# Output projection and the values of two attention branches with 512 moving columns, summed over two halves of the rows

## The chip, the cores and the metric

The kernel runs on one core of a Trainium2 chip. The metric is the device time of one execution in microseconds (us), as the median of several runs; the profile is that of one execution.

## What is computed

One layer of a decoder trunk over 2048 tokens of width 1024, in float32. Cut to what matters here:

```
h    = rmsnorm(x, norm_attn)
proj = h @ w_in                       # 2048x1024 @ 1024x2700, columns split into q, k, v of four branches
o_A  = stick_breaking(qa, ka, va)     # 4 heads of 64: va is 256 columns wide, from column 512
o_B  = native_sparse_attention(...)   # compressed, selected and window parts, gates
o_C  = differential_attention(qc, kc, vc)   # 4 heads, vc is 256 columns wide, from column 1932
o_D  = sliding_window(qd, kd, vd)
mix  = concat(rmsnorm(o_A), rmsnorm(o_B), rmsnorm_per_head(o_C), rmsnorm(o_D))    # 2048x1024
x    = x + (mix * g_mix) @ w_out      # the output projection, 1024x1024
x    = x + relu(rmsnorm(x, norm_mlp) @ w_up)**2 @ w_down
out  = rmsnorm(x, norm_final)
```

## The kernel before

Every float32 product is made of three fp32r products: each operand is split into a high and a low part, and hi\*hi, lo\*hi and hi\*lo are summed in PSUM. So a product over 1024 rows is 8 row blocks of 128 times 3 = 24 matmuls into one PSUM tile.

The tokens go in four chunks c of 512, each of four blocks i of 128. There are two kinds of dense phase. P (`proj`, line 559) projects a chunk with `w_in`; M (`mlp`, line 608) does a chunk's output projection and MLP. The dense stream (`dense`, line 711) runs P0 to P3 and then M0 to M3. The chunk's input, transposed and split, lies in the two tiles `T_hi` and `T_lo`, which `put_T` (line 535) fills block by block.

In P the list `ORDER` (line 62) says which columns follow which. The q and k columns (`MT`) have the weights stationary and `T` moving with 512 columns; the v columns (`NG`) have a block of `T` stationary and the weights moving: 256 columns for `vA` and for `vC`, 268 for `vBD`. Of a v group, ScalarE (`evac`) copies each of the four blocks from PSUM into a tile of the ring `u_lo` (3 buffers), and SP issues the store to `nat_vA`, `nat_vC` or `nat_vBD` in DRAM. `vA` comes first, `vC` tenth in chunk 0 and last in the others, `vBD` last in chunk 0 and before `qD0` in the others.

In M the output projection (lines 620 to 634) takes four passes d of 256 columns. A pass needs two weight tiles of 128x1024, and for each block i it issues 24 matmuls with 256 moving columns; VectorE adds the PSUM tile to `acc`, which holds x (lines 631 and 632). After the last pass a block is normed (`sources`, `norm`), scaled, transposed and put into `T`, and the MLP follows.

Weights come through two `raw` buffers; ScalarE copies the tile to `w_hi`, GpSimd or VectorE subtracts into `w_lo` (`split_weights`, line 411); there are 3 pairs of these (`WB`), held from the first use to the last one of a group. M0 stores the split tiles to DRAM, and M1 to M3 load them from there, without a split, into the three pairs and the two `raw` buffers.

Beside the dense stream runs the attention: scores (PSUM tiles `z`), transposes (`t`), value products (`o`), chunk by chunk in the order A, C, D, B. A planner (`Plan`, `run`) interleaves the streams: it keeps its own estimate of when each operand is ready and issues an attention instruction on TensorE when it is due, and a dense one otherwise. Its price for a matmul is the moving columns divided by 2400 us (line 294): 0.107 us for 256, 0.213 us for 512. M0 begins once all branches of chunk 0 are stored; M3 needs the attention to be over. Dense PSUM tiles (`pd`) have 3 buffers, whatever part of the 512 columns is used.

Of the kernel before, what the change touches and what calls it, by code (L numbers as in the profile page):

```python
# [9 lines left out]
F32 = mybir.dt.float32  # L10
F32R = mybir.dt.float32r
U32 = mybir.dt.uint32
AF = mybir.ActivationFunctionType
OP = mybir.AluOpType
# [5 lines left out]
D = 1024  # L20
# [34 lines left out]
}  # L55

NG = {
    "vA": [(512, 256)],
    "vC": [(1932, 256)],
    "vBD": [(1216, 64), (1344, 76), (2572, 128)],  # L60
}
ORDER = (["vA", "qA0", "qA1", "kA0", "kA1", "qC0", "qC1", "kC0", "kC1", "vC",
# [3 lines left out]


def dap(t, off, dims):
    return bass.AP(tensor=t.tensor, offset=t.offset + off, ap=dims)
# [128 lines left out]
class Trunk:  # L198
# [135 lines left out]
    def weight_specs(self):  # L334
        def w_in(cols, k0, kn):
            wd = sum(w for _, w in cols)
            parts, o = [], 0
            for c0, w in cols:
                def place(t, o=o, w=w):
                    return t[:, :kn * wd].rearrange("p (k w) -> p k w", k=kn)[:, :, o:o + w]  # L340

                parts.append((place, dap(self.w_in, k0 * 128 * IN_COLS + c0,
                                         [[IN_COLS, 128], [128 * IN_COLS, kn], [1, w]])))
                o += w
            return parts

        def up(ft):
            return [(lambda t: t.rearrange("p (k w) -> p k w", k=KD),
                     dap(self.w_up, ft * 128, [[FF, 128], [128 * FF, KD], [1, 128]]))]

        for kind, c in self.phases:
            if kind == "P":
                for m in ORDER[c > 0]:
                    if m in MT:
                        yield kind, c, w_in(MT[m], 0, KD)
                    else:
                        kn = WMAX // sum(w for _, w in NG[m])
                        for k0 in range(0, KD, kn):
                            yield kind, c, w_in(NG[m], k0, min(kn, KD - k0))
            elif c:  # L360
                for j in range(8 + 2 * FF // 128):
                    yield "S", c, j
            else:
                for d in range(4):
                    for kk in range(2):
                        yield kind, c, [(lambda t: t.rearrange("p (k w) -> p k w", k=4),
                                         dap(self.w_out, kk * 512 * D + d * 256, [[D, 128], [128 * D, 4], [1, 256]]))]
                yield kind, c, up(0)
                yield kind, c, up(1)
                for fc in range(FF // 128 // FC):  # L370
                    if FC * fc + 2 < FF // 128:
                        yield kind, c, up(FC * fc + 2)
                    for f in range(FC):
                        yield kind, c, [(lambda t: t, dap(self.w_down, (fc * FC + f) * 128 * D, [[D, 128], [1, D]]))]
                    if FC * fc + 3 < FF // 128:
                        yield kind, c, up(FC * fc + 3)
# [182 lines left out]
    def proj(self, c):  # L559
# [4 lines left out]
        for m in order:  # L564
# [23 lines left out]
            else:  # L588
                wd = sum(w for _, w in NG[m])
                kn = WMAX // wd  # L590
                ws = yield from self.weights(-(-KD // kn))
                ws = [[t.rearrange("p (k w) -> p k w", w=wd) for t in w] for w in ws]
                for i in range(4):
# [11 lines left out]
            self.stored[m] = c  # L605
        self.fill += 1

    def mlp(self, c):

        dn = self.dn  # L610
# [6 lines left out]
            self.ld(a, dap(self.x, (c * 512 + i * 128) * D, [[D, 128], [1, D]]))  # L617
            acc.append(a)
        hh, hl = self.T
        for d in range(4):  # L620
            ws = yield from self.weights(2)
            for i in range(4):
                ts = slice(i * 128, i * 128 + 128)
                ops = []
                for k in range(KD):
                    wh, wl = [w[:, 256 * (k % 4):256 * (k % 4) + 256] for w in ws[k // 4]]
                    ops += [(a[:, k, ts], b) for a, b in ((hh, wh), (hl, wh), (hh, wl))]
                ps = yield from self.group(lambda p: p[:, :256], ops, (i, i + 1), used=d == 3)
                if i == 3:
                    self.res["w"].give(2)  # L630
                a = acc[i][:, d * 256:d * 256 + 256]
                V.tensor_tensor(a, a, ps[:, :256], OP.add)
                if d == 3:
                    self.added[c] = acc[:i + 1]
        self.fill += 1
        us = {}
# [238 lines left out]
    def loads_A(self, c, i, w0):  # L875
        for pr in range(2):
# [2 lines left out]
                yield from self.load_k(("kA", c, pr, j), f"kA{pr}", j, 0, c + 1)  # L879
            yield from self.load_q(("qA", c, pr, 1), f"qA{pr}", i + 2)  # L880
            for j in range(2):
                yield from self.load_v(("vA", c, pr, j), "vA", 128 * pr + 64 * j, 0, c + 1)

    def loads_B(self, c, i, w0):
        for pr in range(2):
# [8 lines left out]
    def loads_C(self, c, i, w0):  # L894
        for h in range(4):
# [2 lines left out]
            for mp in range(2):  # L898
                yield from self.load_k32(("kC", c, h, mp), f"kC{pr}", 2 * j + mp, c + 1)
            yield from self.load_q32(("qC", c, h, 1), f"qC{pr}", 2 * j, i + 2)  # L900
            yield from self.load_v(("vC", c, h), "vC", 64 * h, 0, c + 1)

    def loads_D(self, c, i, w0):
        for pr in range(2):
# [117 lines left out]
    def scores(self):  # L1022
        while self.filled[3] == 0:
            yield None
        self.attention_constants()
        yield from self.await_stored("vA", 0)
        for c in range(NC):
            for g in GROUPS:
                if g == "D":
# [653 lines left out]
```

## Time and profile before

| | us |
|---|---|
| median of 3 runs | 3088.4 (3086.42 to 3092.4) |
| the profiled execution | 3088.61 |
| its span, first instruction to last | 3086.8 |
| TensorE busy | 2995.2 (97%), 18951 matmuls |
| VectorE busy | 1860.2 (60%) |
| ScalarE busy | 1565.2 (51%) |
| mean granted clock | 0.993 of full speed |

A row's busy time of TensorE counts a matmul from its start to its modelled end, about 0.16 to 0.17 us after the next one could start; what a matmul takes of the engine is therefore read from the distance between two starts. "Idle before" is the idle time of the engine just before the instructions of a row, with what ended it.

### The profile page before, as it was taken

The numbers are of one execution on the slowest core, as the hardware profiler recorded it, in microseconds if no ns is written. First come the engines' busy times: TensorE is split into PE (matmuls) and PEld (weight loads), VectorE is DVE, ScalarE is ACT, GpSimd is POOL, SyncE is SP. The second block draws the span as 40 slices with busy tenths as digits, with TensorE's granted clock in tenths as the row PEclk, the third lists the DMA queues.
The fourth block names the chain that finished last, engine by engine and source line by source line (L and its number), as shares of the span: only waits on it lengthen the run. The fifth ranks groups of instructions, "written<-read, shape, count | busy, mean of one in ns | idle before, by whom it ended". The sixth has DMA issues, their size and how long they took to land.

```text
span 3086.8 us, 50946 instructions
## 1 busy us (share of the span) xinstructions
PE 2995.2 (97%) x18951; PEld 2513.8 (81%) x18951; DVE 1860.2 (60%) x4193; ACT 1565.2 (51%) x3195; POOL 449.7 (15%) x397
## 2 busy tenths in 40 slices
PE   8999999999999999999999999999999999999998
PEld 7788887788887777879888777879888888888887
DVE  4665658666656888787554778677654444432323
ACT  4654667554555776655544677545544443221111
POOL 2142323222222222221000000011000000110000
PEclk9999999999999999999999999999999999999999
DMA  7668555669556657877334545565553433645554
GB/s 205 197 202 219 169 165 146 180 185 260 176 195 211 200 183 237 269 243 227 111 139 139 167 148 159 173 198 160 190 158 131 149 123 123 247 163 206 186 204 157
DMA packets 396600, 563.01 MB, mean 182 GB/s; under 512 B 123712, under 2 KB 283584, under 8 KB 394688
## 3 DMA queue, kind: packets, MB, share of 16 engines
q1 hardware_dynamic: 396352, 559.75, 57.0%
q8 instruction: 150, 2.46, 0.3%
q14 instruction: 98, 0.80, 0.1%
HBM read 430.57 MB, written 129.07 MB: 181 GB/s over the span
## 4 chain that ended last, share of the span: by engine, by line
PE 73%; DVE 11%; ACT 7%; DMA 5%; issue 3%; POOL 1%; SPq 1%; DVEq 0%; POOLq 0%; ACTq 0%
PE pdM L296 42%; PE pdP L296 11%; DVE row L117 7%; ACT row L117 4%; PE zB L296 4%; PE tB L300 4%; PE oB L296 4%; PE oC L296 2%; PE tC L300 2%; PE zC L296 2%; DVE acc L117 1%; DMA raw<-in_w_in_dram 1%; DMA out_dram<-acc 1%; PE zD L296 1%; DMA acc<-in_x_dram 1%
## 5 line engine op out<-in xcount | busy, mean ns | idle before, releaser
L117 DVE TENSOR_TENSOR acc<-acc,pdM 128x512 f32<-128x512 f32 (+1 forms) x576 | 372.4, 654 | 229.8 <-PE pdM L296 200.8
L296 PE MATMUL pdM<-T_hi,w_hi 128*128 128x512 f32 (+1 forms) x1040 | 402.2, 387 | 0.7 <-DVE acc L117 0.7
L296 PE MATMUL pdM<-T_lo,w_hi 128*128 128x512 f32 (+1 forms) x1040 | 400.9, 386 | 0.0
L296 PE MATMUL pdM<-T_hi,w_lo 128*128 128x512 f32 (+1 forms) x1040 | 400.5, 385 | 0.0
L117 POOL TENSOR_TENSOR w_lo<-raw,w_hi 128x1024 fp32r<-128x1024 f32 (+2 forms) x92 | 227.7, 2478 | 441.7 <-ACT w_hi L117 375.8
L117 ACT ACTIVATE row<-row 128x1024 f32<-128x1024 f32 (+7 forms) x290 | 229.9, 805 | 108.9 <-DVE row L117 103.5
L296 PE MATMUL pdM<-raw,u_hi 128*128 128x512 f32 x720 | 281.4, 392 | 0.1
L296 PE MATMUL pdM<-w_hi,u_hi 128*128 128x512 f32 x664 | 268.8, 408 | 10.8 <-DVE acc L117 8.1
L296 PE MATMUL pdM<-w_hi,u_lo 128*128 128x512 f32 x664 | 263.8, 397 | 0.0
L296 PE MATMUL pdM<-w_lo,u_hi 128*128 128x512 f32 x664 | 263.3, 397 | 0.2 <-POOL w_lo L117 0.2
L117 ACT ACTIVATE r<-pdM 128x512 f32<-128x512 f32 x128 | 75.9, 593 | 353.3 <-PE pdM L296 351.7
L117 DVE TENSOR_TENSOR u_lo<-r,u_hi 128x512 fp32r<-128x512 f32 x128 | 93.0, 726 | 266.4 <-ACT u_hi L117 266.4
L117 ACT ACTIVATE PT<-tB 128x512 f32<-128x512 f32 (+1 forms) x244 | 130.2, 556 | 192.6 <-PE tB L300 190.9
L296 PEld LDWEIGHTS pdM<-T_hi,w_lo 128*128 128x128 f32 x1040 | 195.9, 188 | 36.7 <-issue 0.2
L296 PEld LDWEIGHTS pdM<-T_hi,w_hi 128*128 128x128 f32 x1040 | 196.0, 188 | 36.6 <-DVE acc L117 0.9
L117 ACT ACTIVATE row<-row,c_mn 128x1024 f32<-128x1024 f32 (+4 forms) x192 | 171.5, 895 | 106.0 <-DVE c_mn L117 104.7
L296 PEld LDWEIGHTS pdM<-T_lo,w_hi 128*128 128x128 f32 x1040 | 196.0, 188 | 35.7 <-issue 0.2
L117 ACT ACTIVATE w_hi<-raw 128x1024 fp32r<-128x1024 f32 (+2 forms) x160 | 164.6, 1036 | 116.9 <-DMA raw<-in_w_in_dram 47.5
L296 PE MATMUL pdP<-T_lo,w_hi 128*128 128x512 f32 x480 | 190.1, 396 | 0.0
L296 PE MATMUL pdP<-T_hi,w_hi 128*128 128x512 f32 x480 | 190.0, 396 | 0.0
L296 PE MATMUL pdP<-T_hi,w_lo 128*128 128x512 f32 x480 | 189.6, 395 | 0.0
L117 ACT ACTIVATE row<-row,b_mw 128x640 f32<-128x640 f32 (+7 forms) x160 | 134.6, 842 | 100.9 <-DVE b_mw L117 97.0
(224 smaller groups left out, 6948.7 us busy)
## 6 DMA issues: line engine op xcount, KB each, us to landing
w_hi<-w SPq DMA_DIRECT2D x162, 512.0 KB, 3.5
w_lo<-w SPq DMA_DIRECT2D x162, 512.0 KB, 4.4
raw<-w SPq DMA_DIRECT2D x108, 512.0 KB, 6.2
raw<-in_w_in_dram SPq DMA_DIRECT2D x72, 512.0 KB, 4.8
w<-w_hi SPq DMA_DIRECT2D x72, 512.0 KB, 3.0
w<-w_lo SPq DMA_DIRECT2D x72, 512.0 KB, 3.8
acc<-in_x_dram SPq DMA_DIRECT2D x32, 512.0 KB, 4.3
raw<-in_w_up_dram SPq DMA_DIRECT2D x32, 512.0 KB, 6.0
```

The costliest lines, as they stand in the source:

```text
L117: return f(*a, **k)
L296: self.nc.tensor.matmul(out, a, b, start=start, stop=stop, **k)
L300: self.nc.tensor.transpose(out, a, self.ident[:a.shape[0], :a.shape[0]])
```

## The change

`vA` and `vC` become one group `vAC` of 512 columns, first in both orders; in the chunks after the first, `vBD` moves to the end. A weight tile of `vAC` holds 2 row blocks of 512 columns (two DMAs of 256 KB) instead of 4 of 256, so the group needs four tiles. It is done in two halves `kh` of the 1024 rows: in the first half each block's 12 matmuls of 512 columns are copied by ScalarE into one of four tiles, two of `u_hi` and two of `u_lo`; in the second half VectorE adds the PSUM tile to that tile, and then it is stored, 512 columns wide.

The output projection takes two passes d of 512 columns, each in two halves of the rows. For each block a half is 12 matmuls of 512 columns instead of 24 of 256, and VectorE adds 512 columns to `acc` each time. The count of passes (4), of weight tiles (8), of PSUM groups (16) and of adds (16) per chunk stays.

```
 NG = {
-    "vA": [(512, 256)],
-    "vC": [(1932, 256)],
+    "vAC": [(512, 256), (1932, 256)],
     "vBD": [(1216, 64), (1344, 76), (2572, 128)],
 }
-ORDER = (["vA", "qA0", "qA1", "kA0", "kA1", "qC0", "qC1", "kC0", "kC1", "vC",
+ORDER = (["vAC", "qA0", "qA1", "kA0", "kA1", "qC0", "qC1", "kC0", "kC1",
           "qB0", "qB1", "kvcmp", "kB", "qD0", "qD1", "kD", "vBD"],
-         ["vA", "kvcmp", "qA0", "qA1", "kA0", "kA1", "qC0", "qC1", "kC0", "kC1",
-          "qB0", "qB1", "kB", "vBD", "qD0", "qD1", "kD", "vC"])
+         ["vAC", "kvcmp", "qA0", "qA1", "kA0", "kA1", "qC0", "qC1", "kC0", "kC1",
+          "qB0", "qB1", "kB", "qD0", "qD1", "kD", "vBD"])
...
-                for d in range(4):
-                    for kk in range(2):
-                        yield kind, c, [(lambda t: t.rearrange("p (k w) -> p k w", k=4),
-                                         dap(self.w_out, kk * 512 * D + d * 256, [[D, 128], [128 * D, 4], [1, 256]]))]
+                for d in range(2):
+                    for kk in range(4):
+                        yield kind, c, [(lambda t: t.rearrange("p (k w) -> p k w", k=2),
+                                         dap(self.w_out, kk * 256 * D + d * 512, [[D, 128], [128 * D, 2], [1, 512]]))]
...
+                if m == "vAC":
+                    yield from self.proj_halves(c, m)
+                    continue
...
+    def proj_halves(self, c, m):
+
+        hh, hl = self.T
+        out = []
+        for kh in range(2):
+            ws = yield from self.weights(2)
+            ws = [[t.rearrange("p (k w) -> p k w", k=2) for t in w] for w in ws]
+            for i in range(4):
+                ts = slice(i * 128, i * 128 + 128)
+                ops = []
+                for k in range(4):
+                    wh, wl = [w[:, k % 2, :] for w in ws[k // 2]]
+                    ops += [(a[:, 4 * kh + k, ts], b) for a, b in ((hh, wh), (hl, wh), (hh, wl))]
+                ps = yield from self.group(lambda p: p, ops, (i, i + 1))
+                if kh == 0:
+                    out.append(self.tile(self.dn, [128, 512], F32R, ("u_hi", "u_lo")[i % 2], 3).bitcast(F32))
+                    self.evac(out[i], ps)
+                else:
+                    self.V.tensor_tensor(out[i], out[i], ps, OP.add)
+                    self.st(self.v_d[m][c * 512 + i * 128:c * 512 + i * 128 + 128, :], out[i])
+            self.res["w"].give(2)
+        self.stored[m] = c
...
-        for d in range(4):
+
+        for d, kh in ((d, kh) for d in range(2) for kh in range(2)):
             ws = yield from self.weights(2)
+            end = d + kh == 2
             for i in range(4):
                 ts = slice(i * 128, i * 128 + 128)
                 ops = []
-                for k in range(KD):
-                    wh, wl = [w[:, 256 * (k % 4):256 * (k % 4) + 256] for w in ws[k // 4]]
-                    ops += [(a[:, k, ts], b) for a, b in ((hh, wh), (hl, wh), (hh, wl))]
-                ps = yield from self.group(lambda p: p[:, :256], ops, (i, i + 1), used=d == 3)
+                for k in range(4):
+                    wh, wl = [w[:, 512 * (k % 2):512 * (k % 2) + 512] for w in ws[k // 2]]
+                    ops += [(a[:, 4 * kh + k, ts], b) for a, b in ((hh, wh), (hl, wh), (hh, wl))]
+                ps = yield from self.group(lambda p: p, ops, (i, i + 1), used=end)
                 if i == 3:
                     self.res["w"].give(2)
-                a = acc[i][:, d * 256:d * 256 + 256]
-                V.tensor_tensor(a, a, ps[:, :256], OP.add)
-                if d == 3:
+                a = acc[i][:, d * 512:d * 512 + 512]
+                V.tensor_tensor(a, a, ps, OP.add)
+                if end:
                     self.added[c] = acc[:i + 1]
```

The rest of the diff renames `vA` and `vC` to `vAC` where the attention loads its values; they are read from one DRAM tensor of 512 columns instead of two of 256.

## Rows read from the trace of the kernel before

**Rows 1.** Page, part 1: busy us (share of the span), instructions of an engine.

```profile
PE 2995.2 (97%) x18951; PEld 2513.8 (81%) x18951; DVE 1860.2 (60%) x4193; ACT 1565.2 (51%) x3195; POOL 449.7 (15%) x397
```

**Rows 2.** Page, part 4: the chain that ended last, shares by engine and line.

```profile
PE 73%; DVE 11%; ACT 7%; DMA 5%; issue 3%; POOL 1%; SPq 1%; DVEq 0%; POOLq 0%; ACTq 0%
```

**Rows 3.** TensorE groups by shape: count, busy us, mean ns, idle before and its releasers.

```profile
L296 PE MATMUL pdM<-w_hi,T_hi 128*128 128x256 f32 x416 | 120.0, 289 | 3.8 <-DVE acc L117 3.7
...
L296 PE MATMUL pdP<-w_hi,T_hi 128*128 128x256 f32 x256 | 76.3, 299 | 6.6 <-DVE acc L117 3.6 <-ACT T_hi L117 2.4 <-DVE u_lo L117 0.6
...
L296 PE MATMUL pdM<-raw,T_hi 128*128 128x256 f32 x192 | 40.3, 285 | 0.6 <-DVE nx L117 0.6
...
L296 PE MATMUL pdM<-raw,T_lo 128*128 128x256 f32 x96 | 27.2, 284 | 0.0
```

**Rows 4.** TensorE timeline, output projection of M3: start us, us, instruction.

```profile
2675.02 0.28 PE L296 MATMUL pdM<-w_hi,T_lo 128*128 128x256 f32 x1
...
2684.02 0.28 PE L296 MATMUL pdM<-w_hi,T_lo 128*128 128x256 f32 x1
```

**Rows 5.** TensorE timeline, q and k columns of P0.

```profile
31.80 0.39 PE L296 MATMUL pdP<-T_hi,w_lo 128*128 128x512 f32 x1
...
53.35 0.39 PE L296 MATMUL pdP<-T_lo,w_hi 128*128 128x512 f32 x1
```

**Rows 6.** Stretches: length, busy us (instructions) of PE, PEld, DVE, ACT, POOL; clock, DMA share, GB/s.

```profile
2676.00:2711.00 35.00, 35.00 (x294) 35.00 (x293) 7.80 (x18) 0.73 (x2) 0.55 (x1) 1.00 0.79 295
2760.00:3040.00 280.00, 280.00 (x1237) 232.03 (x1236) 87.21 (x130) 48.42 (x78) 0.00 (x0) 1.00 0.53 192
0.00:700.00 700.00, 670.20 (x4313) 566.31 (x4314) 443.78 (x1056) 414.12 (x909) 198.26 (x186) 1.00 0.66 186
700.00:2618.00 1918.00, 1873.02 (x12410) 1564.69 (x12409) 1251.23 (x2865) 1060.57 (x2126) 232.81 (x190) 0.99 0.55 179
...
708.00:808.00 100.00, 90.99 (x762) 86.06 (x762) 62.42 (x180) 48.62 (x117) 30.16 (x24) 0.95 0.85 260
```

**Rows 7.** VectorE groups by shape.

```profile
L117 DVE TENSOR_TENSOR acc<-acc,pdM 128x512 f32<-128x512 f32 x512 | 346.0, 684 | 174.5 <-PE pdM L296 172.7
...
L117 DVE TENSOR_TENSOR acc<-acc,pdM 128x256 f32<-128x256 f32 x64 | 26.5, 417 | 55.4 <-PE pdM L296 28.2 <-DMA acc<-in_x_dram 23.6 <-PE pdM L300 3.0
```

**Rows 8.** ScalarE groups by shape.

```profile
L117 ACT ACTIVATE w_hi<-raw 128x1024 fp32r<-128x1024 f32 x148 | 155.0, 1055 | 105.5 <-DMA raw<-in_w_in_dram 44.0 <-PE pdP L296 16.7 <-PE pdM L296 15.9
...
L117 ACT ACTIVATE r<-pdM 128x512 f32<-128x512 f32 x128 | 75.9, 593 | 353.3 <-PE pdM L296 351.7 <-DVE u_lo L117 1.5
...
L117 ACT ACTIVATE u_lo<-pdP 128x256 f32<-128x256 f32 x32 | 11.9, 373 | 0.4 <-PE pdP L296 0.4
```

**Rows 9.** Page, part 5: the split on GpSimd.

```profile
L117 POOL TENSOR_TENSOR w_lo<-raw,w_hi 128x1024 fp32r<-128x1024 f32 (+2 forms) x92 | 227.7, 2478 | 441.7 <-ACT w_hi L117 375.8
```

**Rows 10.** The chain in order of time, 2610 to 2740 us: start us, us, what.

```profile
2624.80 29.96 PE pdM L296 x132
...
2669.49 47.34 PE pdM L296 x378
...
2716.86 0.42 DVE acc L117
```

**Rows 11.** Instructions on the tensor nat_vC: duration ns min/median/max, first and last start us.

```profile
L252 SPq DMA_DIRECT2D nat_vC<-u_lo x16: 319/350/1428, 93.5 to 711.5; - x16
L252 SPq DMA_DIRECT2D v<-nat_vC x16: 366/371/1516, 143.0 to 2103.5; - x16
```

**Rows 12.** Timeline around 508 us, first matmul of the second block of vC, P2.

```profile
508.26 0.39 PE L296 MATMUL pdP<-w_hi,T_hi 128*128 128x256 f32 x1 [0.64 <-DVE u_lo L117]
```

**Rows 13.** Timeline around 170 us, from vBD of P0 to vA of P1.

```profile
170.28 2.82 POOL L117 TENSOR_TENSOR w_lo<-raw,w_hi 128x1024 fp32r<-128x1024 f32 x1
...
171.91 0.39 PE L296 MATMUL pdP<-w_hi,T_hi 128*128 128x256 f32 x1
```

More of the change, by code (lines that the diff above doesn't have):

```diff
@@ L881, in loads_A @@
             for j in range(2):
-                yield from self.load_v(("vA", c, pr, j), "vA", 128 * pr + 64 * j, 0, c + 1)
+                yield from self.load_v(("vA", c, pr, j), "vAC", 128 * pr + 64 * j, 0, c + 1)
     def loads_B(self, c, i, w0):
@@ L900, in loads_C @@
             yield from self.load_q32(("qC", c, h, 1), f"qC{pr}", 2 * j, i + 2)
-            yield from self.load_v(("vC", c, h), "vC", 64 * h, 0, c + 1)
+            yield from self.load_v(("vC", c, h), "vAC", 256 + 64 * h, 0, c + 1)
     def loads_D(self, c, i, w0):
@@ L1025, in scores @@
         self.attention_constants()
-        yield from self.await_stored("vA", 0)
+        yield from self.await_stored("vAC", 0)
         for c in range(NC):
```

## The prediction

> **What bounds the kernel now.** I read the page first: TensorE is busy for 97% of the span [rows 1], and the chain that ended last lies on it for 73%, on VectorE for 11% [rows 2]. A busy share of TensorE is not yet throughput, so the second view is its groups by shape. They give the count of what the change touches: in M the 256-column matmuls with weights moving are the groups on w_hi and T_hi (416, and as many each for the two other products of that pair) and those on `raw` (192 and 96), 3 x 416 + 192 + 96 = 1536; in P they are 3 x 256 = 768 [rows 3]. That is 2304, and the change makes 1152 of 512 columns of them.
>
> The third view is the timeline, where TensorE is full and nothing stands between: 76 matmuls of 256 columns start within 9.00 us, one each 120.0 ns [rows 4]; 96 of 512 columns start within 21.55 us, one each 226.8 ns [rows 5]. The stretches say the same: 294 in 35 us (two or three of them begun before it) and 1237 in 280 us [rows 6]. The 512-column stretch of M3 contains both kinds, weights stationary and weights moving, so 226.7 ns holds for the operands of the new matmuls too.
>
> The last view is the stages. Up to about 2618 us dense work and attention share TensorE, and VectorE is busy for 63 to 65% there [rows 6]; from 2624.8 us the chain is dense work alone, and M3 begins at 2669.5 us [rows 10].
>
> **What is removed on TensorE.** A pair of 256-column matmuls takes 2 x 120.0 = 240.0 ns, the 512-column one 226.7: 13.3 ns less. 1152 x 13.3 = 15.3 us in all: 192 pairs, 2.6 us, in each chunk's output projection, and 96 pairs, 1.3 us, in each chunk's values. The 2.6 us of M3 lie where TensorE never waits [rows 4, 6], so they count in full. The other 12.7 us (7.7 in M0 to M2, 5.1 in P) lie beside the attention. Their lower bound in the ordinary case: of the 2253 us that the chain has on TensorE, M3 takes at most 417, so 1836 of 2669 us before M3, 69%, or 8.8 us. Upper bound: TensorE is busy for 2543 of the first 2618 us, 97%, or 12.3 us [rows 2, 6]. I take the middle, 10.6, since dense work is what fills TensorE when attention isn't ready, which speaks for the upper end, while M0's projection stands beside DMA queues busy for 85% [rows 6], which speaks for the lower.
>
> **What is added on VectorE.** The 64 adds of the output projection grow from 417 to 684 ns: 64 x 267 = 17.1 us, of which 4.3 in M3. The second halves of the values add 16 adds at 684 ns, 10.9 us [rows 7]. ScalarE loses 32 copies at 373 ns and gets 16 of 512 columns; the nearest row from PSUM is 593 ns [rows 8], so 11.9 becomes 9.5 us, a gain of 2.4 that I count as nothing. Before M3 VectorE has 12.8 + 10.9 = 23.7 us more. Bounds: 0 (it is idle for over a third) and 23.7. Queued behind such an add are the row operations of the attention, and for it waits a `pd` buffer that TensorE needs: a block of `vC` waited 0.64 us for VectorE to free one [rows 12]. I take VectorE's part of the chain ahead of M3, 340 of 2669 us or 12.7%: 3.0 us. In M3 only the last add is on the path, where the chain shows it with 0.42 us [rows 10]: plus 0.3.
>
> **What moves.** Three weight pairs, and `vAC` needs two tiles twice in a row. Its fourth tile can be split only when a pair comes free, half a group ahead of the first half's end (6 x 0.2267 = 1.4 us), and it is wanted 1.4 us after that end. The split is 1.06 us on ScalarE and 2.48 on GpSimd [rows 8, 9], so 3.5 - 2.8 = 0.8 us stays open, as it did before from `vC` to the next `vA`. From `vBD` (three tiles) to `vAC` two tiles are missing instead of one, which a second split makes about 1 us later; but the handover from `vBD` to `qD0`, one missing tile wanted at once, is gone. Where such a handover exists before, from `vBD` of P0 to `vA` of P1, the first matmul started 1.6 us into a 2.8 us split, with transposes and attention in between [rows 13]. Net I take 1.0 us; bounds 10.6 us of gain and 21.6 us of loss, both worked out under the rivals.
>
> `vAC` keeps TensorE for 96 x 0.2267 = 21.8 us ahead of `qA0` where `vA` took 96 x 0.12 = 11.5, so the attention of chunk 0 starts some 10 us later. This costs nothing as long as dense work is left when the attention ends: it alone fills the time from 2624.8 to 2669.5 us [rows 10], and of those 45 us the delay, the 3 us of VectorE and the earlier end of the dense work leave about 21. If that cover were gone, each further us would count. The early `vC` brings nothing: its first store was issued at 93.5 us and its first load at 143.0, and the loads go on until 2103.5 us while the stores end at 711.5, so the attention trails the projections and neither `vC` nor the later `vBD` is awaited [rows 11]. SP gets 4 weight DMAs more and 4 stores fewer per chunk, the same bytes; each store now waits for a VectorE add instead of a ScalarE copy, with weight and q/k loads behind it. At 0.684 against 0.373 us that is at most 16 x 0.31 = 5 us; hidden by the prefetched `raw` tiles I take it as 0.
>
> **Sum.** -2.6 - 10.6 + 3.0 + 0.3 + 1.0 = -8.9 us. The profiled execution took 3088.6, 0.2 above the median, and 1.8 of it lie outside its span, which nothing here changes: 3079.7 us.
>
> **Rivals.** (1) *More is gained*: the three handovers from `vBD` to `qD0` each cost a whole split, 3.5 us, and are gone. Then -10.6 more, without the 1.0 and with the upper bound of TensorE: about 3066. For it: GpSimd takes 2.5 to 2.8 us for a split; against: the attention was there to fill the hole [rows 13].
> (2) *The freed time becomes waiting*: before M3 TensorE only waits longer for ScalarE, VectorE and DMA, which hold 27% of the chain, and only M3's part stays: 3088.6 - 2.6 + 0.3 + 1.0 = 3087.
> (3) *The wide matmul saves nothing*: if a 512-column matmul took as long as two narrow ones, only the costs were left, 3088.6 + 4.3 = 3093. Rows 4 to 6 speak against it [rows 4 to 6]. The Trainium skill (TensorE: Matmul & The Clock Gate, Back-to-back issue gap) gives the distance at full clock as the columns over 2.4 GHz plus 2.5 ns. By that a pair would save 2.5 ns and all of them 2.9 us, an estimate from that page, near this rival; the trace disagrees, with 13.3 ns on top of the columns' 106.7 and 213.3.
> (4) *Slower: the weight ring*. Between the halves of `vAC` and behind `vBD` TensorE waits for splits, and the attention doesn't fill it. In full: four halves at 3.5 us and three handovers (into P2, P3 and M0) with a second GpSimd split of 2.48, 14.2 + 7.4 = 21.6 us. With -13.2 and +3.3: 3088.6 + 11.7 = 3100. It is slower than can be told from no change from 6.2 + 13.2 - 3.3 = 16.1 us of such waits on. For it: ScalarE already stood 16.7 us ahead of splits waiting for P's matmuls [rows 8]; against: TensorE's own idle rows in P name no split at all [rows 3].
>
> **How the numbers follow.** 0.2% of 3088.4 is 6.2 us, about what a measurement of this kernel can tell from no change: faster is below 3082.2, slower above 3094.6. The forecast gets 0.52 and a range of its own of 3072 to 3086, since the whole interleave is planned anew with other prices, an unknown that no row bounds; rival 1 0.14, rival 2 0.17, rival 3 0.03, rival 4 0.14. Faster: 0.45 of the forecast and rival 1, 0.59. Same: 0.07 of the forecast, rivals 2 and 3, 0.27. Slower: rival 4, 0.14. The range reaches into rivals 1 and 4, 3063 to 3096, and leaves out about 0.05 below and 0.13 above.
>
> **What would show it.** In the changed profile: 512-column starts 226 to 227 ns apart in M3's output projection, and that projection over in about 43.5 us instead of 46; the 256-column groups with weights moving gone; the adds to `acc` all near 684 ns; attention ending at about 2620 to 2630 us with dense work behind it; no TensorE idle time ended by `w_hi` or `w_lo` in P. The prediction is wrong if TensorE's idle time released by VectorE or by the splits grows by more than 8 us, if the attention ends after the dense work of M2, or if the start distance of the wide matmuls is above 230 ns where TensorE is full.

## The result

| | before | after |
|---|---|---|
| median, us | 3086.69 (6 runs, 3080.77 to 3092.4) | 3116.26 (6 runs, 3114.62 to 3123.01) |
| profiled execution, us | 3088.61 | 3115.1 |
| its span, us | 3086.8 | 3113.4 |

The ratio is 1.0093, interval 1.008 to 1.0107: 29 us slower, where 9 us less was forecast. In the rows PE is TensorE, PEld its weight loads, DVE VectorE, ACT ScalarE, POOL GpSimd and SPq the queue of SP that issues the DMAs. The page's parts 1 and 4 of the changed kernel answer to [rows 1, 2]:

```profile
PE 2996.6 (96%) x17799; PEld 2452.2 (79%) x17799; DVE 1905.6 (61%) x4209; ACT 1567.4 (50%) x3179; POOL 448.9 (14%) x397
...
PE 75%; DVE 11%; ACT 6%; DMA 4%; issue 3%; POOL 1%; SPq 1%; DVEq 0%; POOLq 0%; ACTq 0%
```

1152 matmuls are gone, as they should be, yet the busy time of TensorE has not fallen: a matmul that has a gap behind it shows its modelled end in full, and one at half clock counts nearly double (0.43 us between starts instead of 0.227, below). So the busy total can't say what was saved. The Trainium skill (Perfetto Trace Analysis, Identifying the Most-Contended Engine) says that matmul busy time is not a good measure of how close a kernel is to its limit, because matmuls are pipelined; the trace agrees, with 2995.2 and 2996.6 us for 18951 and 17799 matmuls. Two rows tell more: the group of the `acc` adds, and M3's output projection in the chain in order of time (start, us, what), which answers to [rows 7, 10]:

```profile
L116 DVE TENSOR_TENSOR acc<-acc,pdM 128x512 f32<-128x512 f32 x576 | 388.2, 683 | 209.7 <-PE pdM L295 202.0
```

```profile
2685.74 6.15 DMA out_dram<-acc
2692.48 4.17 DMA nx<-mix_d
2696.69 1.97 PE pdM L299 x8
2698.66 44.84 PE pdM L295 x192
```

192 wide matmuls in 44.84 us; at 226.7 ns each they need 43.5. From 2702.06 us on, 182 of them start 226.7 ns apart on average. What the change does to the instructions came out as worked out. But the projection begins at 2698.66 us, where it began at 2669.49 [rows 10], 29 us later. The rest of M3 runs 25 to 27 us late and has about the same length as before: the whole loss arises ahead of it.

The lines above the projection say where. The timeline of TensorE (start, us, operation, idle before and its releaser) and SP's queue at the same place:

```profile
2679.70 0.27 PE L299 MATMUL tB<-identr,oS 128*128 128x128 f32 x1
2680.98 0.66 PE L299 MATMUL pdM<-identr,nx 128*128 128x128 f32 x4 [1.00 <-DVE scr L116]
2681.99 0.66 PE L299 MATMUL pdM<-identr,nx 128*128 128x128 f32 x4 [0.36 <-DVE nt_ms L116]
2696.69 1.97 PE L299 MATMUL pdM<-identr,nx 128*128 128x128 f32 x8 [14.05 <-DMA nx<-mix_d]
2698.31 0.78 PE L295 MATMUL pdM<-raw,T_hi 128*128 128x512 f32 x1
2698.89 0.63 PE L295 MATMUL pdM<-raw,T_lo 128*128 128x512 f32 x1
```

```profile
2685.32 0.85 SPq L251 DMA_DIRECT2D out_dram<-acc  x2
2687.31 0.33 SPq L251 DMA_DIRECT2D mix_d<-on  x1
2691.95 0.34 SPq L251 DMA_DIRECT2D acc<-in_x_dram  x1
2692.48 0.32 SPq L251 DMA_DIRECT2D nx<-mix_d  x1
```

At 2679.70 the attention issues its last transpose. Its last rows are normed, stored to `mix_d` (2687.31), loaded back (2692.48) and transposed for M3 (2696.69): 17 us from one end to the other, and but for two groups of transposes TensorE has nothing else to do in them. In the kernel before the attention ended at 2618.1 us, dense work of M2 went on until 2674.4, and the wait on that load took 1.29 us:

```profile
2618.14 0.27 PE L300 MATMUL tB<-identr,oS 128*128 128x128 f32 x1
2661.62 1.11 PE L300 MATMUL pdM<-identr,nx 128*128 128x128 f32 x4 [1.29 <-DMA nx<-mix_d]
2674.45 0.39 PE L296 MATMUL pdM<-w_lo,u_hi 128*128 128x512 f32 x1
```

After the hole of the changed kernel the projection's first matmuls start 0.43 us apart instead of 0.227. The stretches (length; busy us of PE, PEld, DVE, ACT, POOL; granted clock, DMA share, GB/s) show the other half of the loss too: between 2640 and 2680 us, where the attention is nearly alone, TensorE is busy for 35 of 40 us.

```profile
2640.00:2680.00 40.00, 35.02 (x293) 26.95 (x292) 22.35 (x50) 24.70 (x50) 4.22 (x5) 1.00 0.12 38
2680.00:2696.00 16.00, 1.31 (x8) 0.84 (x8) 6.53 (x16) 1.99 (x4) 2.48 (x3) 0.63 0.89 316
2696.00:2702.00 6.00, 5.31 (x18) 4.59 (x19) 2.45 (x3) 1.26 (x2) 1.28 (x1) 0.56 0.01 4
2702.00:2740.00 38.00, 38.00 (x169) 31.45 (x169) 10.44 (x16) 2.22 (x4) 0.55 (x1) 1.00 0.47 166
```

Two measures carry the rest of the text. *M2 work left*: the TensorE time of the matmuls from the attention's last instruction to M2's last one (without transposes; up to 2.3 us of M3's first matmuls stand among them). *Waits*: the distance from each TensorE start to the next, less what a matmul of that form takes when nothing is in the way (226.7 ns for 512 columns, 120.0 for 256 [rows 4, 5], 109 for a transpose or 128 columns, 52 for the attention's `o` products; the last two are rough, unbroken runs of them in the trace of before come to 109 and 54.5). Waits so counted include matmuls at half clock. The attention's instructions are the same in all kernels, so what its prices are off by cancels. *Issue time* is the count of matmuls times these prices, as a difference to before; it is worked out and not measured. Each run was timed next to the kernel before on the same chip, whose median there was 3087 to 3092 us; the ratio and "above before" refer to that.

| kernel | ratio to before | issue time, us | M2 work left, us | waits to 700 us | 700 to 2600 | from 2600 |
|---|---|---|---|---|---|---|
| before | | 0 | 47.4 | 65.0 | 160.4 | 11.1 |
| after | 1.0093 | -15.3 | 0 | 70.8 | 165.7 | 41.0 |
| e1 out only | 1.0051 | -10.2 | 8.2 | 69.6 | 168.0 | 29.7 |
| e2 values only | 1.0014 | -5.1 | 43.6 | 69.4 | 167.3 | 10.4 |
| e3 halves narrow | 1.0051 | 0 | 43.4 | 70.2 | 174.5 | 12.9 |
| e4 wide in M3 | 1.0039 | -2.5 | 44.4 | 70.8 | 170.2 | 11.7 |
| e5 narrow M0 | 1.0031 | -7.6 | 36.0 | 70.0 | 173.5 | 12.3 |
| e6 narrow M1 | 0.9964 | -7.6 | 13.4 | 67.8 | 154.4 | 14.3 |
| e7 narrow, half sums | 0.9989 | 0 | 65.1 | 69.1 | 160.9 | 10.3 |
| e8 wide M3 alone | 0.9999 | -2.5 | 48.5 | 66.0 | 162.5 | 11.9 |
| e9 early rows for M3 | 1.0052 | -15.3 | 0 | 72.6 | 168.2 | 27.8 |
| e10 more VectorE | 1.0001 | 0 | 56.7 | 64.3 | 157.1 | 9.9 |
| e11 left 6 us | 1.0037 | -8.9 | 5.4 | 69.5 | 164.1 | 26.6 |
| e12 left 29 us | 0.9972 | -8.9 | 26.7 | 66.7 | 156.3 | 13.1 |
| e13 values and M3 | 1.0044 | -7.6 | 15.2 | 69.7 | 172.5 | 14.4 |
| e14 one quarter, M1 | 0.9976 | -9.5 | 22.2 | 69.5 | 163.4 | 14.5 |
| e15 one quarter, M0 | 1.0007 | -9.5 | 22.2 | 67.1 | 167.4 | 14.8 |
| e16 before again | 0.9999 | 0 | 47.4 | 66.5 | 156.7 | 8.3 |

For the changed kernel, in us: -15.3 of issue time, +29.9 of waits from 2600 us on, +5.8 and +5.3 in the two earlier stretches, 25.7 of the 26.6 us between the spans. The ratio comes from all runs, the waits from one profiled execution each, and those executions lie up to 8 us from their kernel's median. e16, the kernel before once more, gives one example of how far two executions of one kernel differ: 1.5, 3.7 and 2.8 us. (The expectations give the M2 work left as it follows from the kernel's own order of instructions, with M3's first transposes in it, up to 3 us more than the table.)

### The profile page after: what moved, and what is told of

It is laid out like the page before. It is cut to its first block, busy times and chain, and to the rows that moved or that the text cites. A ratio compares the mean times of both kernels' runs of the same rounds, so it can differ in the third digit from the quotient of the medians.

```text
span 3113.4 us, 48653 instructions
## 1 busy us (share of the span) xinstructions
PE 2996.6 (96%) x17799; PEld 2452.2 (79%) x17799; DVE 1905.6 (61%) x4209; ACT 1567.4 (50%) x3179; POOL 448.9 (14%) x397
## 4 chain that ended last, share of the span: by engine, by line
PE 75%; DVE 11%; ACT 6%; DMA 4%; issue 3%; POOL 1%; SPq 1%; DVEq 0%; POOLq 0%; ACTq 0%
PE pdM L295 43%; PE pdP L295 12%; DVE row L116 8%; ACT row L116 4%; PE zB L295 4%; PE tB L299 3%; PE oB L295 3%; PE oC L295 2%; PE zC L295 2%; PE tC L299 2%; DVE acc L116 2%; PE zD L295 1%; DMA row<-kvc_d 1%; ACT PT L116 1%; PE zA L295 1%
## 5 line engine op out<-in xcount | busy, mean ns | idle before, releaser
L116 DVE TENSOR_TENSOR acc<-acc,pdM 128x512 f32<-128x512 f32 x576 | 388.2, 683 | 209.7 <-PE pdM L295 202.0
```

What stands on the lines that cost most here:

```text
L116: return f(*a, **k)
```

## The experiments

**One part alone.** The theory at this point was that work of M2 must be left to lie beside the attention's end and the handover to M3, and that the wide output projection takes it away.

e1 leaves the values as they were: in `ORDER`, `NG`, `proj` and the loads of v, `vA` and `vC` stand as before.

> The wide output projection alone; the values of the first and third branch as before. Theory (the wide projection gets ahead of the attention, so that no dense work of M2 is left to lie beside the attention's last groups and the handover to M3): in this kernel's own order on TensorE the M2 work left behind the attention's last instruction is worth about 9.9 us, against 50.0 in the kernel before and 0 in the changed one. TensorE's issue time is 10.2 us less than before (768 pairs of 256 columns become 768 single ones: 768 x 13.3 ns), and 25 to 35 of the 45 us that the changed kernel lost come back as loss: 3101 to 3112, most of the slowdown. Rival 1 (the joined values, loaded and stored at the head of each block, hold the attention up): about 3077. Rival 2 (the sums in SBUF of the output projection are what holds TensorE up): as long as the changed kernel less what the values gave, 3116 to 3121.

Measured: 3107.89 us, 1.0051 (1.0039 to 1.0063), 15.5 us above before. The hole is there, with 15.91 us ahead of M3's last transposes:

```profile
2692.20 1.97 PE L300 MATMUL pdM<-identr,nx 128*128 128x128 f32 x8 [15.91 <-DMA nx<-mix_d]
```

Rival 1 is out as the main cause, and rival 2's 3116 to 3121 were not reached. In the expected range, but for a reason only half right: 18.6 us of the added waits lie from 2600 us on, 12.2 ahead of it.

e2 leaves the output projection as it was: in `weight_specs` and `mlp`, four passes of 256 columns as before.

> The values of the first and third branch joined to 512 columns and the new order of the groups; the output projection as before. Theory: 46.2 us of M2 work are left behind the attention's last instruction, near the 50.0 of before, so the gain in issue time (384 x 13.3 ns = 5.1 us) stays: 3080 to 3085. Rival 1 (the joined values hold the attention up): 3095 to 3110, most of the slowdown. Rival 2 (the sums of the output projection): 3080 to 3085 as well, so this run doesn't part it from the theory.

Measured: 3096.82 us, 1.0014 (1.0005 to 1.0024), 4.4 us above before; expected were 3080 to 3085, which lies below before on any chip (3092 on this one), so the expectation failed. The handover is sound (10.4 us of waits from 2600 on), but the 5.1 us of issue time don't show: the waits ahead of 2600 us are 11.3 us longer. The values give nothing back, and cost little.

e3 keeps the halves and the wide adds and takes the wide matmul away:

```
-                ps = yield from self.group(lambda p: p, ops, (i, i + 1), used=end)
+                ps = None
+                for q in range(2):
+                    ps = yield from self.group(lambda p, q=q: p[:, 256 * q:256 * q + 256],
+                                               [(x, y[:, 256 * q:256 * q + 256]) for x, y in ops], (i, i + 1), ps, q == 1, end and q == 1)
```

> The output projection summed over two halves of the rows with VectorE adds of 512 columns and the changed weight tiles, as in the changed kernel, but each matmul of 512 columns issued as two of 256 into the halves of the same PSUM tile; values as before. Theory: the width of the matmul is what lets the projection get ahead; here 46.0 us of M2 work are left behind the attention, and no issue time is saved: 3084 to 3092, the time of before. Rival 2 (the 512-column sums on VectorE, the halves and the weight tiles cost the time): 3105 to 3120. Rival 1 says the time of before.

Measured: 3108.1 us, 1.0051 (1.0036 to 1.0066), 15.7 us above before. The theory's 3084 to 3092 failed. Rival 2's 3105 to 3120 held as it stands; against the 3088 of before that it was written for it means 17 us and more above before, and the 15.7 fall just short of that. The handover is in order (43.4 us left, 12.9 of waits); what is longer are the waits before, by 5.2 up to 700 us and 14.1 from there to 2600. So a second thing costs time, one that the theory didn't have.

e4 is e3 with `if c < 3:` around the narrow form:

> As the one with narrow matmuls (halves, adds of 512 columns, changed weight tiles; values as before), but with 512-column matmuls in M3, where the attention is over. Theory: 47.0 us of M2 work are left behind the attention, and M3's projection loses 192 x 13.3 ns = 2.6 us on the path that sets the end: 2 to 4 us below the kernel with narrow matmuls everywhere, 3081 to 3089. Rival 2: 3105 to 3120. If the wide matmul itself were at fault wherever it stands, this kernel would be above the narrow one.

Measured: 3102.89 us, 1.0039 (1.0027 to 1.0051), 5.2 below e3 where 2 to 4 were expected. Against e3 the wide matmul in M3 is a gain. As a time of its own neither expectation held: the theory had 3081 to 3089, rival 2 3105 to 3120.

**The cover, with the same instructions.** The next runs differ only in which chunk's or which part's matmuls stay narrow. That hardly changes the issue time, but it changes the order on TensorE, and with it the M2 work left.

e5 has `if c == 0:` around the narrow form, e6 `if c == 1:`.

> The output projection over two halves of the rows, with matmuls of 512 columns in M1 to M3 and pairs of 256 in M0; values as before. 576 pairs become single ones, 7.7 us of issue time less than before. Theory (work of M2 left behind the attention's last instruction is what counts): 38.7 us of it are left, so the wait at the handover from M2 to M3 stays small; from the kernel with narrow matmuls everywhere, which stood 15.7 us above before, it comes down by the issue time: 6 to 14 us above before. Rival (only the sums over halves and their VectorE adds cost time, the order doesn't): the same as with M1 narrow.

> The same with the pairs of 256 columns in M1 in place of M0: the same instructions in number and size, the same 7.7 us of issue time saved, but in its order only 16.0 us of M2 work are left behind the attention's last instruction. Theory: 14 to 24 us above before, 6 to 14 above the kernel with M0 narrow, and the difference stands in a wait between the last group of M2 and the projection of M3. Rival (sums and adds): no difference between the two beyond 2 us, both about 8 us above before.

Measured: e5 3099.64 us, 1.0031 (1.0019 to 1.0044), as expected; e6 3079.68 us, 0.9964 (0.9951 to 0.9976), 20 us *below* e5 where the theory had it 6 to 14 above, and the lowest ratio of all runs: this expectation failed. 13.4 us of M2 work turned out to be enough for the handover: its longest wait on the load is 2.63 us.

```profile
2654.29 1.11 PE L300 MATMUL pdM<-identr,nx 128*128 128x128 f32 x4 [2.63 <-DMA nx<-mix_d]
```

And e5, with 36 us left, has 19.1 us more waits between 700 and 2600 us. The stretches of e5 and then e6 (columns as above) show it as TensorE's idle time, 52.1 and 39.3 us:

```profile
700.00:2600.00 1900.00, 1847.92 (x11826) 1521.01 (x11826) 1261.42 (x2858) 1050.88 (x2110) 236.67 (x191) 0.99 0.55 179
```

```profile
700.00:2600.00 1900.00, 1860.72 (x11888) 1533.20 (x11888) 1278.95 (x2865) 1051.73 (x2111) 231.79 (x191) 0.99 0.56 181
```

The cover counts only below some point, and the second thing is worth as much.

e11 and e12 stand on either side of that point, with 96 pairs narrow in M1 each: `if c == 1 and d == 0:` and `if c == 1 and kh == 0:`.

> The output projection over two halves with 512-column matmuls, but pairs of 256 in M1 for the first 512 columns (both halves of the rows); values as before. 672 pairs become single ones: 8.9 us of issue time less than before. Only 5.9 us of M2 work are left behind the attention's last instruction. Theory: the handover to M3 waits some 25 us between 2600 and 2720 us, 15 to 19 more than before: 2 to 20 us above before, and 8 to 18 above the next kernel. Rival (small waits alone): no difference to the next kernel.

> The same number of pairs of 256 columns, in M1 for the first half of the rows (both halves of the columns): the same instructions and the same 8.9 us of issue time saved, but 29.4 us of M2 work left behind the attention. Theory: no more wait at the handover than before (6 to 9 us between 2600 and 2720): from 10 us below before to 8 above, the spread being what small waits in M0 to M2 do. Rival: the same as the one before it.

Measured on one chip: e11 3099.43 us, 1.0037 (1.0025 to 1.0049); e12 3079.6 us, 0.9972 (0.9961 to 0.9983). Twenty us between two kernels of the same instructions, in the order that the theory had, each within its range against before; the distance is a little above the 8 to 18 us expected. The stretch from 2600 to 2740 us of both, and of before (columns as above):

```profile
2600.00:2740.00 140.00, 121.03 (x707) 100.93 (x707) 61.51 (x117) 41.67 (x82) 12.87 (x14) 0.93 0.47 170
```

```profile
2600.00:2740.00 140.00, 132.91 (x733) 111.87 (x733) 61.05 (x106) 35.76 (x70) 16.15 (x17) 0.98 0.53 193
```

```profile
2600.00:2740.00 140.00, 134.04 (x880) 119.84 (x875) 54.73 (x101) 32.36 (x63) 16.07 (x17) 0.98 0.55 197
```

TensorE idles for 19.0 us in e11 and 7.1 in e12, 6.0 in before; the wait on the load ahead of M3 is 15.69 us in one row of e11 and 1.54 in e12. The waits from 2600 us on differ by 13.5 of the 24.0 us between the spans; 7.8 lie between 700 and 2600, 2.8 ahead.

e14 and e15 put back only 48 of e1's 768 pairs: `if (c, d, kh) == (1, 1, 0):` and `(0, 1, 0)`.

> The output projection alone (values as before) with 512-column matmuls, but for one of the four parts of M1 (second 512 columns, first half of the rows): 48 pairs of 256, 0.64 us more issue time than the kernel with all of them wide, which stood 0.51% above before. 24.8 us of M2 work are left behind the attention instead of 9.9. Theory: 2600 to 2740 waits 11 to 14 us instead of 24; 10 below to 6 above before, 10 to 25 below the kernel with all wide. Rival (the gain of the last kernels came from their narrow matmuls as such, in proportion to their number): 8 to 14 above before.

> The same with the 48 pairs in M0 (second 512 columns, first half of the rows). 25.2 us of M2 work are left behind the attention. Theory: as the one with the quarter in M1, 10 below to 6 above before; the two may differ by the small waits in M0 to M2. Rival: 8 to 14 above before.

Measured: e14 3084.41 us, 0.9976 (0.9966 to 0.9985); e15 3093.04 us, 1.0007 (0.9996 to 1.0018). With 0.64 us *more* issue time they are 0.75% and 0.44% below e1: in both the waits from 2600 on fall from 29.7 to under 15, and both lie in the theory's range. Of TensorE's waits in that stretch (who waited for whom, us in total, times, longest) e1 has the first of these lines, e14 the second:

```profile
PE pdM L300 <- DMA nx<-mix_d: 17.8, 2, 15.9
```

```profile
PE pdM L300 <- DMA nx<-mix_d: 4.1, 1, 4.1
```

The rival, gain in proportion to the narrow matmuls, is out. (With the same M2 work left, e14 and e15 still stand 0.31% apart; that part is not explained.)

**The handover itself.** e9 is the changed kernel, with M3's rows taken from chunk 2:

```
-                t0 = c * 512 + i * 128
+                m = 2 if (kind, c) == ("M", 3) else c
+                t0 = m * 512 + i * 128
                 if kind == "M":
-                    while self.mix_n[4 * c + i] < 7:
+                    while self.mix_n[4 * m + i] < 7:
```

> The changed kernel, but M3's output projection takes the mixed rows of chunk 2 in place of those of chunk 3, which are stored long before: the wait on the attention's last group, its norm, its store and the load behind it falls away (the result of chunk 3 is another). The order on TensorE stays nearly the same: no M2 work lies behind the attention's last instruction. Theory: the 14.05 us hole in front of M3's transposes and the 3 to 4 us at half clock behind it go, the thin stretch without dense work before it stays: 12 to 18 us below the changed kernel, about 3098 to 3106 where before is at 3088. Rival (the slowdown is made of small waits all over the kernel): no change beyond 4 us.

Measured: 3104.72 us, 1.0052 (1.0039 to 1.0065), some 13 us below the changed kernel by the ratios, as the theory had it. Its waits from 2600 us on fall by 13.2 us, in the earlier stretches they don't. The chain (start, us, what) goes from M2's last add through one split of `T` to M3's projection, with no load in it, and the projection's first matmul starts at 2686.72 us instead of 2698.31, though the attention ended 6 us later (2686.1):

```profile
2684.61 0.75 DVE acc L116
2686.74 1.29 POOL T_lo L116
2688.08 2.79 PE pdM L295 x11
2690.87 0.87 PE pdM L299 x8
2691.74 40.85 PE pdM L295 x180
```

The hole is shown. What remains from 2600 us on are 16.7 us of waits above before; some 13 of them lie between 2620 and 2690 us, where the attention runs nearly without dense work beside it. That this lack of dense work makes them was not tested by itself.

**Joined values with cover.** e13 is the changed kernel with the narrow form under `if c < 3:`.

> The changed kernel (joined values, halves, adds of 512 columns) with the output projection's matmuls in pairs of 256 columns in M0 to M2 and 512 only in M3: 576 pairs and the values' 384 become... of the 1152 that the change saves 576 are saved, 7.7 us of issue time less than before. 17.8 us of M2 work are left behind the attention's last instruction, 0 in the changed kernel. Theory: the waits between 2600 and 2740 us fall from 35.3 to 11 to 15, and the time from 29 above before to between 6 below and 12 above. Rival (joined values at the head of each block hold the attention up by themselves): 15 to 25 above before.

Measured: 3103.45 us, 1.0044 (1.0029 to 1.0059): 13.6 us above before by the ratio (12.3 by the medians), just past the theory's 12 and short of the rival's 15. The part that the theory speaks of came as said, 14.4 us of waits from 2600 on instead of 41.0; what kept the kernel from gaining are 12.1 us more between 700 and 2600.

**The second thing: is it VectorE?** e7 (first) is e3 with half of each sum left out, e10 (second) is the kernel before with a VectorE pass more:

```
-                a = acc[i][:, d * 512:d * 512 + 512]
-                V.tensor_tensor(a, a, ps, OP.add)
+                a = acc[i][:, d * 512:d * 512 + 256]
+                V.tensor_tensor(a, a, ps[:, :256], OP.add)
```

```
                 V.tensor_tensor(a, a, ps[:, :256], OP.add)
+                V.tensor_scalar(a, a, 1.0, None, op0=OP.mult)
```

> As the kernel with narrow matmuls everywhere (halves, changed weight tiles, 15.7 us above before), but each sum in SBUF takes only the first 256 of its 512 columns: the other half of the output projection's columns is left out of the result. 64 VectorE adds of 417 ns in place of 64 of 684, the VectorE time of before. 67.7 us of M2 work are left behind the attention. If the adds' time on VectorE (17 us more) is what costs the narrow kernel its 15.7 us: within 4 us of before. If it is the halves and the new order of the groups with them: still 10 to 18 us above before.

> The kernel before with one more VectorE pass over the 256 columns (times 1.0) behind each of the output projection's 64 adds: more VectorE time than the changed sums bring (64 passes of some 0.3 us, about 19 us, in bounds of 10 and 27), the same issue time on TensorE, and 59.3 us of M2 work left behind the attention. If VectorE's time stands in the attention's way one for one, as the kernel with half sums lets think (17 us less VectorE time, 19 us less time): 10 to 27 us above before. If it is the order of the work on TensorE that moves the small waits, and not the VectorE time: within 5 us of before.

Measured: e7 3087.25 us, 0.9989 (0.998 to 0.9999), which alone would speak for the adds: 17 us less VectorE time, 19 us less in all. But its order changed with the adds too. e10: 3089.03 us, 1.0001 (0.9992 to 1.0011), with this in the page's part 1:

```profile
PE 2991.2 (97%) x18951; PEld 2508.4 (81%) x18951; DVE 1885.1 (61%) x4257; ACT 1565.1 (51%) x3195; POOL 446.9 (15%) x397
```

VectorE is busy for 24.9 us more than in before (20.5 of them the new passes) and the time is the same. VectorE's time by itself isn't the cost. Another reading is left open by these two runs: the wider adds hold a PSUM buffer 0.27 us longer each, which e7 takes away and e10 does not bring. TensorE's waits in M that ended with a write of VectorE to `acc`, those adds among them (us in total, times, longest), before and then e3, speak against it, since they have not grown:

```profile
PE pdM L296 <- DVE acc L117: 12.4, 12, 2.7
```

```profile
PE pdM L296 <- DVE acc L117: 9.9, 8, 2.0
```

e8 is the kernel before with only M3's projection wide, its tiles read back from the stored narrow ones in two parts each:

> The kernel before in everything up to M2; in M3 alone the output projection with 512-column matmuls over two halves, its weight tiles read back from the stored ones in two parts each. 51.1 us of M2 work are left behind the attention's last instruction. Theory: nothing in front of M3 changes, M3's projection is 192 x 13.3 ns = 2.6 us shorter on the path that sets the end: 1 to 4 us below before, and 10 to 14 below the kernel that has halves in M0 to M2 as well. Rival (the halves cost time wherever they stand, M3 too): 1 to 5 us above before.

Measured: 3089.42 us, 0.9999 (0.9989 to 1.0009). 2.5 us less issue time, and no gain that can be told; the waits grew by 3.9 us, no more than two executions of one kernel differ by. The theory's 1 to 4 us below before and the rival's 1 to 5 above both miss; the theory's 10 to 14 below e4 came, with 12. The interval ends at 1.0009, 3 us above before: most of the 12 us that e4 lies above before are therefore not in M3 but come with the halves in M0 to M2.

**How much is chance.** e16 is the kernel before, unchanged.

> The kernel before, unchanged, with a second profile. The time of before within 2 us. Its waits on TensorE by stretch tell what two executions of one kernel differ by: if P0's 65.0 us of waits stay within 1 us, then the 70 us of the other kernels come from their order; if they come to 68 to 70, it is the execution. The same for the 160 us between 700 and 2600.

Measured: 3091.72 us, 0.9999 (0.9989 to 1.0009). Its waits are in the table; the 66.5 us up to 700 us lie between the two cases of the expectation. One repeat is a thin measure, but the 9.8 to 14.1 us that e3, e4, e5 and e13 have more between 700 and 2600 us are well above it, and the ratios of these kernels stand above 1 by intervals clear of it: they are hardly chance. The 5 us that the changed kernel has more there are little above it.

What they are made of stays open. The clock doesn't explain them: between 700 and 2600 us TensorE stood at the lower of its two levels (1.2 and 2.4 GHz) for 27.3 us in before and for 27.3 in e5, which waits 13.1 us more there. In e3 the list of waits gives many small ones: among these waits of TensorE between 700 and 1500 us (who waited for whom, us in total, times, longest) none comes to more than 5.3 us in total, and those on VectorE, ScalarE and loads have all grown or shrunk a little against before.

```profile
PE pdM L296 <- DVE acc L117: 5.3, 4, 2.0
PE zB L296 <- DVE b_mw L117: 4.2, 3, 2.0
PE pdM L296 <- DVE u_lo L117: 2.7, 1, 2.7
PE pdM L296 <- ACT r L117: 2.7, 3, 1.7
```

The four with 170 us or more there have M0's projection in narrow matmuls over halves, and e6 and e12, with M0 wide and narrow ones in M1, have 154 to 156; but e7 has it narrow too, at 160.9, and e1 has it wide, at 168.0. No property of the kernels that was tried sorts these waits, and no run held the order still while it changed a size.

## Why the prediction was wrong

**Right:** the instruction level. Wide starts are 226.7 ns apart in M3 against 240.0 for a narrow pair, so 13.3 ns for each, and 1152 pairs became single matmuls: 15.3 us less to issue. 683 ns for the add (684 in [rows 7]), and M3's projection waiting for nothing once the clock is up.

**Right in kind, small:** waits of P for the split. The forecast's rival 4 had up to 21.6 us of them; in the changed kernel TensorE waits 3.6 us for `w_hi`, once. That rival's time, 3100, was on the correct side by another mechanism than the one that acted.

**Right in size, without a visible price:** VectorE. Worked out were 17.1 + 10.9 = 28.0 us more. The changed adds came to 16.7 + 10.9; the pages differ by 45.4, and the rest stands in rows of the attention whose count is the same, above all the 64 scalings `onC<-onC,gc_rs` (22.0 us before, 33.1 after) and the 64 of `c_cc` (15.9 and 22.5). Why these took longer is open. In e10 24.9 us more cost nothing, so no run shows the 3.0 us in the sum as a price of VectorE's time.

**The step that failed:** the cover. "of those 45 us the delay, the 3 us of VectorE and the earlier end of the dense work leave about 21", and "attention ending at about 2620 to 2630 us". It ended at 2679.7 us and left nothing. The step took the order of before and moved its two ends by the microseconds saved or added. But the order is planned anew, and M2's end barely moved (2674.4 to 2679.5 us) while the attention's moved by 61.6 us: the dense work ran ahead in the first 2600 us and the attention fell behind (at 2600 us the attention still had 4.7 us of TensorE time to issue in the kernel before and 44.7 in the changed one, at the prices above), and at the end it stood without dense work beside it. How far can't be had from sums of durations: 48 narrow pairs out of 768 change the M2 work left from 8.2 to 22.2 us. The text said that each further microsecond would count if the cover were gone, and named as a sign of error that the attention ends after M2's dense work; it gave that case no price and no chance. It had one: the chain from the attention's last transpose to M3's first matmul, some 17 us in the changed kernel, plus the attention's end alone. Together they made 29.9 us more of waits, twice what the wide matmuls save.

**Also wrong:** that most of the 12.7 us saved beside the attention would come through as time (10.6 was taken). In the changed kernel the waits ahead of 2600 us grew by 11.1 us, of which e16 lets some 5 be chance. e2 and e8 save 5.1 and 2.5 us with the handover in order and show no gain. Rival 2, the freed time becomes waiting, describes these two; e6 and e12 gain what they save, e14 most of it. Which of the two it is goes with the order; by what mechanism is open.

## What to carry to other kernels

Where two streams are interleaved on one engine and the next stage needs the end of one of them, the work of the other that is left behind that end is a term of its own: price the handover (here norm, store, load, transpose, some 17 us) and ask what lies beside it. Here it cost little where 13 us or more were left (8 to 15 us of waits from 2600 us on, 11.1 in before) and nearly in full at 8 us and less (one wait of 14 to 16 us in the changed kernel, e1 and e11); nothing between 8 and 13 was measured. A change that speeds up the filling stream can use up its own cover, so look at the two ends in the new kernel's order before trusting the sum; here keeping a few narrow matmuls in M1 (e6, e12) turns 0.5% of loss into 0.3 to 0.4% of gain, faster than both kernels compared.

## What the runs showed of the hardware

A hole of 14 us on TensorE costs more than its length: the granted clock was 0.63 on average in the 16 us from 2680 and 0.56 in the next 6, near the lower of its two levels, so the first matmuls behind the hole started 0.43 us apart instead of 0.227 until about 2701 us, some 1.3 us on top of M3's projection. The Trainium skill (TensorE: Matmul & The Clock Gate, HAM oscillation — how this bites in real kernels) tells of the same: a wait on a load long enough for the clock to fall makes the next work start at half clock; the trace agrees, with 0.56 behind the 14.05 us hole. Much shorter waits go either way. In before, TensorE waited 1.54 and 1.29 us ahead of M3; in e16, the same kernel, 1.54 and 1.32. In before the clock fell and was 0.50 from 2661 to 2665 us, in e16 it stayed at 1.00, which makes up most of the 2.8 us between their waits from 2600 us on (before, then e16; columns as above):

```profile
2661.00:2665.00 4.00, 3.38 (x10) 2.79 (x11) 0.96 (x4) 1.37 (x4) 1.15 (x2) 0.50 0.68 230
```

```profile
2661.00:2665.00 4.00, 4.00 (x24) 3.40 (x23) 4.00 (x6) 1.71 (x4) 1.15 (x1) 1.00 0.32 119
```

The load ahead of the last transposes took 4.2 us, but it was issued on SP 5.2 us after the store that it reads from. That store took 4.9 us to land, in a stretch where the DMA engines were busy for 0.89 of the time; two `out_dram` stores, one of them 6.15 us long in the chain, lay ahead of both, and the last of them landed only 0.3 us earlier. Whether the handover would be shorter without them was not tested.
